# Encoder layer on one core: two weight sums of every seven-product pair made by GpSimd instead of VectorE

## The chip, the core and the metric

One core of a Trainium2 chip runs the whole layer. The metric is the device time of one execution in microseconds (us), the median of three runs. In views of the profile PE is TensorE's matmul side and PEld its weight loads, DVE is VectorE, ACT is ScalarE, POOL is GpSimd, SP is the queue that issues the large loads. All tiles of this kernel have 128 partitions; "128x512" is 512 float32 elements on each.

## The reference

A post-LN encoder layer on 256 tokens of width 2048: LayerNorm, one input projection, two kinds of attention, an output projection with residual and LayerNorm, a SwiGLU FFN of width 5632, residual and a last LayerNorm. What the change touches are the three FFN matrix products:

```python
    h = layer_norm(DEEPNORM_ALPHA * h + mixed, ln1_g[l], ln1_b[l])
    ffn = jnp.einsum('bsf,fd->bsd', jax.nn.silu(jnp.einsum('bsd,df->bsf', h, w_gate[l]))
                     * jnp.einsum('bsd,df->bsf', h, w_up[l]), w_down[l])
    h = layer_norm(DEEPNORM_ALPHA * h + ffn, ln2_g[l], ln2_b[l])
```

## The kernel before

**Precision by splitting.** A float32 operand is split into a rounded high part (`fp32r`, written by ScalarE) and a low part (value minus high part, written by VectorE). One product is then three matmuls: high by high, high by low, low by high. So each weight tile that TensorE takes costs ScalarE a copy and VectorE a subtraction.

**Seven products.** Activations and weights of two successive k-blocks (a "pair": raw tiles r1 and r2 of 128x1024, each halved into two blocks of 512 columns) form a 2x2 by 2x2 block product. Most groups make it of eight block products. In the pairs listed in `SEVEN` and `SEVEN_D` it is made of seven, by a Strassen-Winograd scheme, which needs four sums of weight blocks before the splits. `seven_parts` lists the eleven operations of such a pair:

- `t1` = r1 left + r1 right, and `t3` = r1 right + r2 right, both 128x512, written to the two halves of one tile `t`;
- `t24`: two more sums that read `t` and r2, each 128x512;
- `hi11`, `split_hi`, `hi13`, `hi24`: high parts by ScalarE; `lo11` (128x512), `lo2`, `lo13`, `lo24` (128x1024 each): low parts by VectorE. `hi13` and `lo13` read `t`.

Seven-product pairs are 4 of the 8 pairs of each of ten FFN groups (five "gate" and five "up" groups of 1024 columns, taken in turns: one gate and one up group are a period below) and 12 of the 44 pairs of the down projection, 52 in all. A pair of seven products is 21 matmuls of 128x512, one of eight is 24.

**Order.** Every engine runs its own instructions in the order in which they were emitted, and waits by semaphores. The emission order is made by a planner in the kernel (`Timed`, `Step`, `next_part`): it walks the list of products that TensorE shall take, keeps a clock for each engine with reckoned costs, and emits part operations of the pairs ahead as soon as their engine's reckoned clock is near TensorE's. For GpSimd it reckons `0.1 + n / 400` us, for VectorE `0.07 + n / 960` (n elements per partition). All weight and work tiles come from one pool of 46 slots of 4 KB per partition (`SLOTS`).

**GpSimd's own work.** In the FFN its queue holds only the stores of the FFN's middle activations to DRAM (`mid_d`, from tile `nb`): two 512-column blocks for each of two token tiles per period, each after TensorE has transposed the block and ScalarE has copied it out. They come back as operands of the down projection. Earlier GpSimd makes the reciprocal square roots of the LayerNorms (`rsqrt`: a `TENSOR_SCALAR`, then a `TENSOR_TENSOR` power, tile `rstd`) and issues small loads.

The operations are recorded by a helper class, so that nearly every row of the profile names its line, L53. Rows are told apart by engine, tiles and shape. Buffers of the slot pool are called `sl`, accumulators in PSUM `acc`.

Of the kernel before, what the change touches and what calls it, by code (L numbers as in the profile page):

```python
# [12 lines left out]
ALU = mybir.AluOpType  # L13
# [239 lines left out]
def layer_kernel(ctx: ExitStack, tc: tile.TileContext, A: dict, out: bass.AP):  # L253
    nc = Timed(tc.nc)
# [17 lines left out]
    def slot(shape, dt=F32):  # L272
        t = slab.tile(shape, dt, tag="slab", name=nm("sl"))
        if len(taken) + len(left_over) >= SLOTS and left_over:
            old = min(left_over, key=lambda x: nc.idle(x))
            left_over.remove(old)
            nc.follows(t, old)
        taken.append(t)
        return t
# [5 lines left out]
    def leave(*tiles):  # L285

        for t in tiles:
            taken.remove(t)
            left_over.append(t)
# [3 lines left out]
    def used(key, n, *tiles):  # L293

        uses[key] = uses.get(key, 0) + 1
        if uses[key] == n:
            leave(*tiles)
# [109 lines left out]
    def split_hi(u):  # L407
        wh[u] = slot([P, 1024], F32R)
        nc.scalar.activation(wh[u], raw[u], AF.Copy)

    def split_lo(u):
        wl[u] = slot([P, 1024], F32R)
        nc.vector.tensor_tensor(wl[u], raw[u], wh[u].bitcast(F32), op=ALU.subtract)
# [590 lines left out]
    def op(engine, fn, reads=(), after=(), early=False, takes=0):  # L1004


        return dict(engine=engine, fn=fn, reads=reads, after=after, early=early, takes=takes, done=False)
# [13 lines left out]
    def seven_parts(u):  # L1021

        r1, r2 = raw[u], raw[u + 1]
        s = sums[u] = {}

        def t1():
            s["t"] = slot([P, 2, 512])
            nc.vector.tensor_tensor(s["t"][:, 0], r1[:, :512], r1[:, 512:], op=ALU.add)

        def t3():  # L1030
            nc.vector.tensor_tensor(s["t"][:, 1], r1[:, 512:], r2[:, 512:], op=ALU.add)

        def hi11():
            s["b11"] = slot([P, 2, 512], F32R)
            nc.scalar.activation(s["b11"][:, 0], r1[:, :512], AF.Copy)

        def lo11():
            nc.vector.tensor_tensor(s["b11"][:, 1], r1[:, :512], s["b11"][:, 0].bitcast(F32), op=ALU.subtract)
            leave(r1)

        def hi13():
            s["hi"], s["lo"] = slot([P, 2, 512], F32R), slot([P, 2, 512], F32R)
            nc.scalar.activation(s["hi"], s["t"], AF.Copy)

        def lo13():
            nc.vector.tensor_tensor(s["lo"], s["t"], s["hi"].bitcast(F32), op=ALU.subtract)
            used(("t", u), 2, s["t"])

        def t24():
            s["u"] = slot([P, 2, 512])  # L1050
            nc.vector.tensor_tensor(s["u"][:, 0], s["t"][:, 0], r2[:, 512:], op=ALU.add)
            nc.vector.tensor_tensor(s["u"][:, 1], s["u"][:, 0], r2[:, :512], op=ALU.add)
            used(("t", u), 2, s["t"])
            used(("r2", u), 2, r2)

        def hi24():
            s[2], s[4] = slot([P, 2, 512], F32R), slot([P, 2, 512], F32R)
            nc.scalar.activation(s[2], s["u"], AF.Copy)

        def lo24():  # L1060
            nc.vector.tensor_tensor(s[4], s["u"], s[2].bitcast(F32), op=ALU.subtract)
            leave(s["u"])

        def lo2():
            split_lo(u + 1)
            used(("r2", u), 2, r2)

        return [
            op("act", hi11, lambda: [r1], takes=1),
            op("dve", t1, lambda: [r1], takes=1),  # L1070
            op("dve", t3, lambda: [r1, r2], (1,)),
            op("act", lambda: split_hi(u + 1), lambda: [r2], takes=1),
            op("dve", lo11, lambda: [s["b11"][:, 0]], (0, 1, 2)),
            op("act", hi13, lambda: [s["t"]], (1, 2), takes=2),
            op("dve", t24, lambda: [s["t"]], (1, 2), takes=1),
            op("dve", lo2, lambda: [wh[u + 1]], (3,), takes=1),
            op("act", hi24, lambda: [s["u"]], (6,), takes=2),
            op("dve", lo13, lambda: [s["hi"]], (5,)),
            op("dve", lo24, lambda: [s[2]], (8,)),
        ]  # L1080
# [370 lines left out]
    def prepare(u, seven):  # L1451

        if u not in stages:
            stages[u] = seven_parts(u) if seven else one_parts(u)
            if splits_mid(u):
                add_mid_split(u, stages[u])
            if seven and is_down(u):
                add_mid_sums(u, stages[u])
        return stages[u]
# [165 lines left out]
```

## Time and profile before

| | us |
|---|---|
| median of three runs (lowest, highest) | 1127.96 (1127.65, 1128.34) |
| the profiled execution, its device time | 1127.88 |
| span from its first to its last instruction | 1126.1 |
| FFN with seven-product pairs, from the span's start | 440 to 880.55 |
| down projection | 880.55 to 1086 |
| one gate group and one up group | 83.5 |

The profiled execution's time is its span and 1.8 us around it, and it is 0.08 us from the median. A matmul's duration in the profile overlaps that of the next one, so its start-to-start distance or the count in a stretch tells TensorE's pace, not its busy time. VectorE's records overlap a little in the same way: a record lasts longer than the distance to the next one's start. In the views of stretches overlaps are counted once.

### The profile page before, as it was taken

The page shows a single profiled execution, that of the slowest core. Times are in us where ns is not written, and L with a number is a line of the kernel's source. Part 1 is how long each engine was busy: PE and PEld are TensorE (multiplying, and loading weights), DVE is VectorE, ACT ScalarE, POOL GpSimd, SP SyncE. Part 2 cuts the span into 40 slices and gives each one's busy share as a digit, 9 for nine tenths or more (in the row PEclk, how much of TensorE's full clock was granted, in tenths as well). Part 3 has the DMA queues.
Part 4 walks back from the last instruction along what each step waited for, and adds up shares of the span by engine and source line. Part 5 has one row for each costly group of instructions (what it writes and reads, how often), then busy time and mean ns, then how long its engine had stood idle before and what let it go on. Part 6 is the DMA issues. An engine that isn't in the chain of part 4 may idle for free.

```text
span 1126.1 us, 14151 instructions
## 1 busy us (share of the span) xinstructions
PE 1111.5 (99%) x5032; PEld 904.7 (80%) x5032; DVE 929.0 (83%) x1263; ACT 598.9 (53%) x785; POOL 57.7 (5%) x110
## 2 busy tenths in 40 slices
PE   8999999999999999999999999999999999999998
PEld 4788888888788876888888888888888788878885
DVE  7863876547773669999999999999999999799865
ACT  5552656435563228656556556556567566446640
POOL 2000003110100020000000000000000000000000
PEclk9999999999999999999999999999999999999999
DMA  9664548795766754655754755755756877667741
GB/s 345 233 202 157 166 145 166 183 205 190 159 220 229 243 183 135 211 195 174 269 205 165 278 204 164 280 193 177 271 208 222 286 266 279 218 225 283 250 166 75
DMA packets 70407, 237.15 MB, mean 211 GB/s; under 512 B 8516, under 2 KB 9924, under 8 KB 70336
## 3 DMA queue, kind: packets, MB, share of 16 engines
q1 hardware_dynamic: 65008, 220.49, 57.2%
q0 software_dynamic: 5168, 15.68, 6.8%
q8 instruction: 39, 0.64, 0.2%
q14 instruction: 32, 0.26, 0.1%
q10 hardware_dynamic: 160, 0.08, 0.0%
HBM read 226.25 MB, written 9.97 MB: 210 GB/s over the span
## 4 chain that ended last, share of the span: by engine, by line
PE 49%; issue 41%; DVE 4%; ACT 2%; POOL 2%; DMA 1%; POOLq 0%; ACTq 0%; DVEq 0%
PE acc L53 49%; DVE sl L53 3%; POOL mid_d L53 1%; ACT sl L53 1%; DMA mid_d<-nb 1%; DVE stats L53 1%; ACT s L53 1%; DMA ident<-in_c_ident_dram 0%; DVE s L53 0%; POOL h_d L53 0%; POOL rs L53 0%; DMA sl<-in_w_out_dram 0%; POOL rstd L53 0%; ACT o L53 0%; DVE o L53 0%
## 5 line engine op out<-in xcount | busy, mean ns | idle before, releaser
L53 PE MATMUL acc<-sl,sl 128*128 128x512 f32 (+1 forms) x4676 | 1063.0, 388 | 2.3 <-DVE sl L53 1.4
L53 PEld LDWEIGHTS acc<-sl,sl 128*128 128x128 f32 x4676 | 860.5, 188 | 184.1 <-issue 6.2
L53 DVE TENSOR_TENSOR sl<-sl,sl 128x1024 fp32r<-128x1024 f32 (+3 forms) x710 | 683.1, 1017 | 44.9 <-ACT sl L53 36.6
L53 ACT ACTIVATE sl<-sl 128x1024 fp32r<-128x1024 f32 (+1 forms) x530 | 498.6, 994 | 272.8 <-DVE sl L53 140.8
L53 ACT ACTIVATE sl<-acc 128x256 fp32r<-128x256 f32 (+2 forms) x70 | 33.1, 497 | 91.0 <-PE acc L53 72.4
L53 DVE TENSOR_TENSOR sl<-acc,sl 128x256 fp32r<-128x256 f32 (+2 forms) x94 | 54.8, 596 | 28.2 <-ACT sl L53 21.5
L53 DVE TENSOR_TENSOR sl<-sl 128x512 f32<-128x512 f32 (+1 forms) x76 | 41.4, 558 | 0.3 <-PE acc L53 0.3
L53 DVE SCALAR_TENSOR_TENSOR sl<-sl,acc 128x512 f32<-128x512 f32 x10 | 6.8, 679 | 36.6 <-PE acc L53 36.6
L53 POOL DMA_DIRECT2D mid_d<-nb x22 | 11.9, 540 | 459.1 <-ACT nb L53 459.1
L53 ACT COPY sl<-acc 128x512 f32<-128x512 f32 x31 | 17.1, 588 | 34.3 <-PE acc L53 34.3
L53 ACT COPY nb<-acc 128x512 f32<-128x512 f32 x24 | 14.1, 588 | 35.1 <-PE acc L53 30.3
L53 DVE TENSOR_SCALAR sl<-acc 128x512 f32<-128x512 f32 x8 | 5.5, 688 | 32.7 <-PE acc L53 32.7
L53 ACT ACTIVATE s<-s 128x512 f32<-128x512 f32 x20 | 12.3, 631 | 23.5 <-DVE s L53 23.5
L53 ACT ACTIVATE s<-s,mx 128x256 f32<-128x256 f32 x32 | 15.9, 499 | 15.4 <-DVE mx L53 15.4
L53 POOL DMA_DIRECT2D nb<-in_na_rpb_dram x32 | 19.6, 621 | 85.7 <-DVE s L53 85.7
L53 PE MATMUL acc<-ident,s 128*128 128x128 f32 x136 | 20.5, 273 | 2.5 <-DVE s L53 1.7
L53 PEld LDWEIGHTS acc<-ident,s 128*128 128x128 f32 x136 | 16.5, 140 | 7.5 <-issue 1.9
L53 DVE TENSOR_TENSOR sl<-sl,acc 128x512 f32<-128x512 f32 x16 | 10.6, 681 | 12.7 <-PE acc L53 12.7
L53 PEld LDWEIGHTS acc<-ident,sl 128*128 128x128 f32 x128 | 15.2, 140 | 6.4 <-issue 4.5
L53 DVE BATCH_NORM_STATS2 stats<-sl 128x6 f32<-128x512 f32 x24 | 16.4, 692 | 3.2 <-DMA sl<-in_x_dram 2.6
L53 DVE SCALAR_TENSOR_TENSOR sl<-sl,rstd,sl 128x512 f32<-128x512 f32 x21 | 15.8, 752 | 3.5 <-POOL rstd L53 1.9
L53 DVE SCALAR_TENSOR_TENSOR sl<-sl,mv,sl 128x512 f32<-128x512 f32 x24 | 17.7, 745 | 0.2
(82 smaller groups left out, 226.2 us busy)
## 6 DMA issues: line engine op xcount, KB each, us to landing
sl<-in_w_in_dram SPq DMA_DIRECT2D x96, 512.0 KB, 4.8
sl<-in_w_down_dram SPq DMA_DIRECT2D x88, 512.0 KB, 5.8
sl<-in_w_gate_dram SPq DMA_DIRECT2D x80, 512.0 KB, 4.3
sl<-in_w_up_dram SPq DMA_DIRECT2D x80, 512.0 KB, 4.5
sl<-in_w_out_dram SPq DMA_DIRECT2D x32, 512.0 KB, 5.1
sl<-mid_d SPq DMA_DIRECT2D x14, 512.0 KB, 4.1
mid_d<-nb POOLq DMA_DIRECT2D x22, 256.0 KB, 3.4
sl<-in_w_gate_dram SPq DMA_DIRECT2D x16, 256.0 KB, 4.2
```

The lines of the kernel that those rows point to most:

```text
L53: result = getattr(self.engine, op)(*args, **kw)
```

## The change

`t1` and `t3` of every seven-product pair are issued to GpSimd, and the planner's list names `pool` as their engine, so that it reckons them at GpSimd's cost and on GpSimd's clock. The operands, the tile `t` and the eleven operations stay.

```diff
         def t1():
             s["t"] = slot([P, 2, 512])
-            nc.vector.tensor_tensor(s["t"][:, 0], r1[:, :512], r1[:, 512:], op=ALU.add)
+            nc.gpsimd.tensor_tensor(s["t"][:, 0], r1[:, :512], r1[:, 512:], op=ALU.add)
 
         def t3():
-            nc.vector.tensor_tensor(s["t"][:, 1], r1[:, 512:], r2[:, 512:], op=ALU.add)
+            nc.gpsimd.tensor_tensor(s["t"][:, 1], r1[:, 512:], r2[:, 512:], op=ALU.add)
...
             op("act", hi11, lambda: [r1], takes=1),
-            op("dve", t1, lambda: [r1], takes=1),
-            op("dve", t3, lambda: [r1, r2], (1,)),
+            op("pool", t1, lambda: [r1], takes=1),
+            op("pool", t3, lambda: [r1, r2], (1,)),
```

104 rows leave VectorE's queue (1202 rows before, 1098 now) and join GpSimd's (88 before, 192 now); the other engines keep their numbers of rows.

GpSimd's queue before, where the second period's four stores stand (names are out<-in; `nb` is the copied block):

```order
L53 DMA mid_d<-nb_4821 128x512
L53 DMA mid_d<-nb_5456 128x512
L53 DMA mid_d<-nb_5495 128x512
L53 DMA mid_d<-nb_5522 128x512
L53 DMA mid_d<-nb_5559 128x512
L53 DMA mid_d<-nb_6194 128x512
```

The same place now, from the last pair of one up group to the second pair of the next gate group:

```order
L53 TENSOR_TENSOR sl_5379<-sl_5341 128x512
L53 TENSOR_TENSOR sl_5379<-sl_5341,sl_5343 128x512
L53 DMA mid_d<-nb_5449 128x512
L53 DMA mid_d<-nb_5476 128x512
L53 TENSOR_TENSOR sl_5495<-sl_5431 128x512
L53 TENSOR_TENSOR sl_5495<-sl_5431,sl_5433 128x512
L53 DMA mid_d<-nb_5514 128x512
L53 DMA mid_d<-nb_5543 128x512
L53 TENSOR_TENSOR sl_5595<-sl_5560 128x512
```

The sums `t1` and `t3` of a pair (same output tile, twice) now stand between the stores and after them.

VectorE's queue before, at one seven-product pair in that place (r1 is `sl_5428`, r2 `sl_5430`, `t` is `sl_5511`):

```order
L53 TENSOR_TENSOR sl_5511<-sl_5428 128x512
L53 TENSOR_TENSOR sl_5511<-sl_5428,sl_5430 128x512
L53 TENSOR_TENSOR sl_5483<-sl_5428,sl_5483 128x512
L53 TENSOR_TENSOR sl_5529<-sl_5511,sl_5430 128x512
L53 TENSOR_TENSOR sl_5529<-sl_5529,sl_5430 128x512
L53 TENSOR_TENSOR sl_5549<-sl_5430,sl_5485 128x1024
L53 TENSOR_TENSOR sl_5540<-sl_5511,sl_5539 128x1024
L53 TENSOR_TENSOR sl_5570<-sl_5529,sl_5569 128x1024
```

VectorE's queue now, at the same pair (r1 `sl_5431`, r2 `sl_5433`, `t` `sl_5495`):

```order
L53 TENSOR_TENSOR sl_5493<-sl_5431,sl_5493 128x512
L53 TENSOR_TENSOR sl_5520<-sl_5495,sl_5433 128x512
L53 TENSOR_TENSOR sl_5520<-sl_5520,sl_5433 128x512
L53 TENSOR_TENSOR sl_5532<-sl_5433,sl_5498 128x1024
L53 TENSOR_TENSOR sl_5530<-sl_5495,sl_5529 128x1024
L53 TENSOR_TENSOR sl_5547<-sl_5520,sl_5546 128x1024
```

`t1` and `t3` are gone from the head of the piece; `lo11` leads it, and the second row, the first sum of `t24`, now waits for GpSimd.

## Rows read from the trace of the kernel before

**Rows 1.** The page's busy time, share of the span and instructions of each engine.
```profile
PE 1111.5 (99%) x5032; PEld 904.7 (80%) x5032; DVE 929.0 (83%) x1263; ACT 598.9 (53%) x785; POOL 57.7 (5%) x110
```
**Rows 2.** Stretches: length, busy us and starts of each engine, granted clock, DMA share, GB/s.
```profile
424.00:428.00 4.00, 3.83 (x10) 1.52 (x8) 3.96 (x10) 4.00 (x7) 0.00 (x0) 1.00 0.02 8
...
440.00:880.55 440.55, 440.55 (x1980) 364.25 (x1979) 432.43 (x524) 263.68 (x309) 9.72 (x18) 1.00 0.63 216
...
548.41:631.95 83.54, 83.54 (x378) 69.12 (x377) 81.89 (x99) 49.49 (x59) 2.16 (x4) 1.00 0.61 214
...
880.55:1086.00 205.45, 203.42 (x900) 167.17 (x899) 188.66 (x245) 115.42 (x128) 4.30 (x8) 1.00 0.73 255
```
**Rows 3.** Waits from 440 to 880.55: us in total, times, longest.
```profile
POOL mid_d L53 <- ACT nb L53: 378.8, 18, 80.2
...
DVE sl L53 <- ACT sl L53: 2.6, 5, 0.5
DVE sl L53 <- PE acc L53: 2.3, 5, 0.5
...
PEld acc L53 <- DVE sl L53: 0.4, 2, 0.3
```
**Rows 4.** Waits from 880.55 to 1086.
```profile
DVE sl L53 <- PE acc L53: 8.6, 5, 3.7
DVE sl L53 <- ACT sl L53: 7.1, 9, 1.6
```
**Rows 5.** VectorE from 440 to 880.55 by shape: count, busy us, mean ns of one, idle before.
```profile
L53 DVE TENSOR_TENSOR sl<-sl,sl 128x512 f32<-128x512 f32 x123 | 84.5, 687 | 1.4
...
L53 DVE TENSOR_TENSOR sl<-sl 128x512 f32<-128x512 f32 x41 | 28.1, 684 | 0.0
L53 DVE TENSOR_TENSOR sl<-acc,sl 128x512 f32<-128x512 f32 x30 | 20.7, 689 | 2.8 <-PE acc L53 2.3
L53 DVE TENSOR_TENSOR o<-acc,sl 128x512 f32<-128x512 f32 x19 | 13.0, 686 | 0.5
L53 DVE TENSOR_TENSOR s<-acc,sl 128x512 f32<-128x512 f32 x20 | 12.9, 683 | 0.1
```
**Rows 6.** VectorE in order of time from 562 to 575: start, us, operation.
```profile
564.06 0.69 DVE L53 TENSOR_TENSOR sl<-sl 128x512 f32<-128x512 f32 x1
564.66 8.29 DVE L53 TENSOR_TENSOR sl<-sl,sl 128x512 f32<-128x512 f32 x9
```
**Rows 7.** VectorE and GpSimd in order of time from 404 to 406.5.
```profile
404.57 0.75 DVE L53 SCALAR_TENSOR_TENSOR sl<-sl,mv,sl 128x512 f32<-128x512 f32 x1
404.63 0.74 POOL L53 TENSOR_SCALAR rstd<-mv 128x1 f32<-128x1 f32 x1 [56.39 <-DVE mv L53]
```
**Rows 8.** The same two engines from 18.3 to 19.5.
```profile
18.28 0.63 DVE L53 TENSOR_TENSOR sl<-acc,sl 128x512 fp32r<-128x512 f32 x1
...
18.45 0.19 POOL L53 TENSOR_SCALAR rstd<-mv 128x1 f32<-128x1 f32 x1 [8.11 <-DVE mv L53]
...
18.73 0.55 POOL L53 TENSOR_TENSOR rstd<-rstd,mhalf 128x1 f32<-128x1 f32 x1
...
18.82 0.74 DVE L53 SCALAR_TENSOR_TENSOR sl<-sl,mv,sl 128x512 f32<-128x512 f32 x1
```
**Rows 9.** GpSimd in order of time, two more of the five TENSOR_SCALAR rows.
```profile
414.20 0.74 POOL L53 TENSOR_SCALAR rstd<-mv 128x1 f32<-128x1 f32 x1 [6.47 <-DVE mv L53]
...
1106.37 0.74 POOL L53 TENSOR_SCALAR rstd<-mv 128x1 f32<-128x1 f32 x1 [78.98 <-DVE mv L53]
```
**Rows 10.** GpSimd at the start: the only 128x512 operation it makes, and a 128x1.
```profile
0.72 0.52 POOL L53 MEMSET nb<- 128x512 f32 x1 [0.29 <-POOLq L1610]
1.18 0.10 POOL L53 MEMSET mhalf<- 128x1 f32 x1
```
**Rows 11.** GpSimd from 540 to 645: one period's stores and the next one's first.
```profile
548.41 0.54 POOL L53 DMA_DIRECT2D mid_d<-nb  x1 [80.19 <-ACT nb L53]
552.29 0.54 POOL L53 DMA_DIRECT2D mid_d<-nb  x1 [3.35 <-ACT nb L53]
555.54 0.54 POOL L53 DMA_DIRECT2D mid_d<-nb  x1 [2.71 <-ACT nb L53]
558.87 0.54 POOL L53 DMA_DIRECT2D mid_d<-nb  x1 [2.79 <-ACT nb L53]
631.95 0.54 POOL L53 DMA_DIRECT2D mid_d<-nb  x1 [72.54 <-ACT nb L53]
```

## The prediction

> **What bounds the kernel now.** I read the page's busy shares first [rows 1]: PE is busy 99% of the span, VectorE 83%, GpSimd 5%. On that page the change looks free: work leaves a loaded engine for an idle one. The share over the span misleads, so I then read the stretches in which the moved operations stand [rows 2]. From 440 to 880.55, the FFN, VectorE is busy 432.43 of 440.55 us; 8.1 us are idle, 2%. In the same stretch PE starts 1980 matmuls (transposes among them) in 440.55 us, one in 0.2225 us, and one period of 83.54 us has 378, one in 0.221 us. The pace is constant, so TensorE sets the time. The third view, the waits of that stretch [rows 3], says the same: TensorE waited 0.4 us for VectorE, VectorE 2.3 us for TensorE's accumulators and 2.6 us for ScalarE. So TensorE is the bound and VectorE follows it almost without slack. The reader is to see two things in this. Taking work off VectorE can give back no more than TensorE loses now. Adding work of more than 2% to VectorE makes it the bound. In the down projection (880.55 to 1086) VectorE idles 205.45 - 188.66 = 16.8 us, nearly all of it waiting for TensorE (8.6) and ScalarE (7.1) [rows 4], and TensorE loses 205.45 - 203.42 = 2.0 us.
>
> **What the change removes.** 52 pairs lose two 128x512 additions each on VectorE. A `t1` row starts at 564.06 and the next row at 564.66 [rows 6], so one costs VectorE 0.60 us; its record of 0.68 overlaps the next. 41 of the `t1` rows stand in the FFN stretch [rows 5], 11 behind it. VectorE is relieved of 82 x 0.60 = 49.2 us in the first stretch and 22 x 0.60 = 13.2 us in the second. If that were all, TensorE would gain at most 0.4 us in the first and 2.0 us in the second.
>
> **What it adds to GpSimd.** The trace has no large two-input operation on GpSimd. Nearest rows: a memset of 128x512 takes 0.52 us, one of 128x1 takes 0.10 [rows 10], so a stream of 512 elements per partition costs 0.42; an operation on a tiny tile with an input and an output takes 0.19 when nothing hinders it [rows 8]. An addition reads two such streams and writes one. If the write hides beside the reads, it is 0.19 + 2 x 0.42 = 1.03 us; if all three come after one another, 0.19 + 3 x 0.42 = 1.45 us. I take the middle, 1.24. Even 104 x 1.45 = 151 us are little for an engine that is busy 9.72 + 4.30 = 14 us in the 646 us of both stretches [rows 2]. GpSimd's own time is therefore not the question.
>
> **What it does to VectorE: the step that decides.** In [rows 7] GpSimd's `TENSOR_SCALAR` of 128x1 starts 0.06 us into a VectorE operation with two SBUF inputs, lasts 0.74 us and ends at 405.37, 0.05 us after that operation's end at 405.32. The same instruction takes 0.19 in [rows 8], where VectorE was busy too, but with one of its inputs from PSUM. [Rows 9] have 0.74 twice more. So the two engines share a way into SBUF; a VectorE operation with two SBUF inputs holds it until it ends, and GpSimd waits. What no row shows is the other direction, since every GpSimd operation here reads one or two elements per partition: the VectorE row at 18.82 began beside one and lasted its usual 0.74 [rows 8]. I infer that a way held exclusively by one is also held against it by the other, for as long as GpSimd streams its inputs. Then each moved addition does not relieve VectorE of 0.60 us but takes its time on GpSimd out of VectorE's two-SBUF work. VectorE can meanwhile do only what reads PSUM: 71 rows, 20.7 + 13.0 + 12.9 us and two more rows of 1.4, together 48 of 432 us, 11% [rows 5]. So a moved addition of G us costs VectorE 0.89 G and saves it 0.60. If instead VectorE always won the way, the bill would be alike: its next row in the queue, `t24`, waits for `t`, and it would stand idle there while GpSimd makes both sums.
>
> [...]
>
> **The sum.** FFN: 82 x (0.89 x 1.24 - 0.60) = 41.3 us of new work for VectorE, less the 8.1 us that it idles: TensorE is held up by 33.2 us. Down projection: 22 x 0.504 = 11.1 us, of which I let half of the 16.8 us of idle time take 8.4 (its waits do not lie where the seven-product pairs do): 2.7 us. Together 35.9 us on the profiled 1127.88, 1163.8 us; that execution is 0.08 us from the median, which I neglect. With G at 1.03: 82 x 0.317 - 8.1 = 17.9, and nothing in the down projection: 1146. With G at 1.45: 82 x 0.69 - 8.1 = 48.5 and 22 x 0.69 - 8.4 = 6.8: 1183. If VectorE finds no PSUM work to do while it waits, G at 1.24 gives 82 x 0.64 - 8.1 + 22 x 0.64 - 8.4 = 50, 1178.
>
> **Costed at nothing.** ScalarE's `hi13` now waits for GpSimd; ScalarE is busy 263.68 of 440.55 us [rows 2], and if that cover failed, `lo13` and `lo24` would come late, which is inside the same VectorE bill. Weight loads stay where they are on SP's queue (the same 441 rows) and follow freed slots. TensorE's clock: it is granted 1.00 even from 424 to 428, where only 10 matmuls start in 4 us [rows 2], so short stalls should not cost clock.
>
> **The rivals.**
> *One-way way in.* GpSimd waits for VectorE, but VectorE never for GpSimd, and GpSimd slips in between VectorE's operations. Then an addition is late by at most one VectorE operation and done within some 2.5 us, which the look-ahead covers; VectorE has 49.2 us more room, TensorE keeps its pace: 1127.9, no change. For it: the row at 18.82 was not delayed. Against it: that GpSimd operation read one element, so there was nothing to delay. It decides if VectorE's rows beside GpSimd's additions keep their durations; the border between loss and none is G = (0.60 + 8.1 / 82) / 0.89 = 0.79 us.
> *Relief.* The same, and VectorE's room removes what TensorE loses now: 2.4 us at most, 1125.5.
> *GpSimd's queue.* VectorE is not hindered, but the sums stand behind the stores of `mid_d`, as the order shows, and these wait for ScalarE's copies, 378.8 us in 18 waits [rows 3], 2.7 to 3.4 us apart within a period [rows 11]. Two pairs per period have their sums behind a store. If VectorE stood at `t24` for one such distance for each, it would be 5 x 2 x 2.7 = 27 us; since the planner emits ahead, I price it at half of that, 13 us: 1141. Against it: from 440 to 880.55 VectorE has 49 us of freed time to make such a stall up, and the stall must be longer than the look-ahead.
>
> **How the numbers follow.** Exclusive both ways, 0.80, 1163.8 with its own range 1144 to 1190; one-way, 0.12, 1127.9; the queue alone, 0.05, 1141; relief, 0.03, 1125.5. A change under 0.2%, 2.3 us, is about what three runs of this kernel cannot tell from none. The forecast's own range leaves out some 0.08 (both bounds of G lie in it, the extreme of 1.45 without any PSUM work does not: 82 x 0.85 - 8.1 + 22 x 0.85 - 8.4 = 72, 1200). To leave out no more than 2 in 10 it must reach the one-way case: 1127 to 1190. Relief counts half to faster and half to the same, so faster 0.02, same 0.13; the rest, 0.85, is slower.
>
> **What the next profile would show.** Right: GpSimd has 104 `TENSOR_TENSOR` rows of 128x512 of about 1.0 to 1.5 us, or longer where they include the wait; VectorE's 128x1024 subtractions beside them last longer than 1219 ns or have gaps of about G before them; a period grows from 83.5 to about 90 us with TensorE's waits for VectorE at some 6 us in each; VectorE is idle or stretched, although it has 104 operations less. The gate and up periods carry nearly all of the loss, the projections and attention before 440 none. Wrong: periods of 83.5 us with VectorE's busy time down by 9.6 us in each (one-way), VectorE waiting mostly for GpSimd rows that themselves wait for `nb` (queue), or additions on GpSimd of well over 1.5 us, which would put the time over 1190.

## The result and the profile after

The changed kernel takes 1168.34 us (median of four runs, 1167.22 to 1170.14), against 1127.81 for the kernel before (1127.56 to 1128.34). The ratio is 1.0358, with a 95% interval of 1.0345 to 1.0371. The profiled execution took 1167.22 us with a span of 1165.4, 39.3 us more than before. One execution of one experiment below, the last, ran at a granted clock of 0.556 and took 1883.71 us; it is in a slow state and left out.

The page's line of busy shares, which answers to [rows 1]:

```profile
PE 1128.4 (97%) x5032; PEld 910.9 (78%) x5032; DVE 966.0 (83%) x1159; ACT 600.6 (52%) x785; POOL 251.5 (22%) x214
```

VectorE makes 104 operations less and is busy 37 us more. That is the result in one line. The same stretches as in [rows 2], moved to where they now lie (FFN, its second period, down projection):

```profile
440.00:916.58 476.58, 456.25 (x1986) 370.66 (x1985) 462.23 (x442) 265.01 (x309) 161.61 (x101) 0.98 0.58 201
556.50:646.36 89.86, 86.21 (x378) 69.94 (x377) 87.68 (x83) 49.91 (x58) 31.30 (x20) 0.98 0.57 199
916.58:1125.00 208.42, 203.46 (x893) 166.90 (x892) 195.51 (x222) 115.82 (x128) 43.83 (x30) 0.99 0.72 251
```

The FFN is 476.58 - 440.55 = 36.0 us longer, the down projection 208.42 - 205.45 = 3.0, and the end 0.3; nothing is lost before 440. VectorE's idle time in the FFN is 476.58 - 462.23 = 14.4 us, 3% of the stretch, and TensorE's idle time there is 476.58 - 456.25 = 20.3 us where it had none: VectorE now sets the time, and no longer TensorE.

VectorE in the FFN by shape, as in [rows 5] (count, busy us, mean ns, idle before). First the row of the kernel before for 1024 columns, then the changed kernel's:

```profile
L53 DVE TENSOR_TENSOR sl<-sl,sl 128x1024 fp32r<-128x1024 f32 x214 | 248.0, 1219 | 2.6 <-ACT sl L53 2.6
...
L53 DVE TENSOR_TENSOR sl<-sl,sl 128x1024 fp32r<-128x1024 f32 x214 | 310.2, 1503 | 8.4 <-ACT sl L53 8.2
L53 DVE TENSOR_TENSOR sl<-sl,sl 128x512 f32<-128x512 f32 x82 | 68.9, 840 | 1.4
L53 DVE TENSOR_TENSOR sl<-sl,sl 128x512 fp32r<-128x512 f32 x45 | 34.0, 755 | 0.0
L53 DVE TENSOR_TENSOR sl<-acc,sl 128x512 f32<-128x512 f32 x30 | 20.5, 685 | 1.8 <-PE acc L53 1.0 <-ACT sl L53 0.5
L53 DVE TENSOR_TENSOR o<-acc,sl 128x512 f32<-128x512 f32 x19 | 13.0, 684 | 0.1
```

Of these groups those that read only SBUF are longer (1024 columns: 1219 ns before, 1503 now; the 512-column sums: 687 before, 840 now). The rows that read PSUM kept their 0.68 to 0.69 us. The new rows of GpSimd in the same stretch, `t1` and `t3`:

```profile
L53 POOL TENSOR_TENSOR sl<-sl 128x512 f32<-128x512 f32 x41 | 80.9, 1974 | 226.4 <-PE acc L53 115.0 <-DVE sl L53 59.4 <-DMA sl<-in_w_up_dram 40.7
L53 POOL TENSOR_TENSOR sl<-sl,sl 128x512 f32<-128x512 f32 x41 | 74.3, 1813 | 20.6 <-DMA sl<-in_w_up_dram 13.7 <-DMA sl<-in_w_gate_dram 5.9 <-DMA sl<-in_w_down_dram 1.0
```

These means hold waiting inside an instruction: unhindered, a sum takes 1.28 to 1.30 us. One place shows both engines in order of time (start, us). First GpSimd, where two sums run unhindered from 560.27 and two hindered from 570.50:

```profile
559.71 0.54 POOL L53 DMA_DIRECT2D mid_d<-nb  x1 [2.65 <-ACT nb L53]
560.27 1.30 POOL L53 TENSOR_TENSOR sl<-sl 128x512 f32<-128x512 f32 x1
561.53 1.28 POOL L53 TENSOR_TENSOR sl<-sl,sl 128x512 f32<-128x512 f32 x1
...
570.50 2.18 POOL L53 TENSOR_TENSOR sl<-sl 128x512 f32<-128x512 f32 x1 [3.60 <-DMA sl<-in_w_gate_dram]
572.63 2.29 POOL L53 TENSOR_TENSOR sl<-sl,sl 128x512 f32<-128x512 f32 x1
```

And VectorE beside them:

```profile
559.99 3.91 DVE L53 TENSOR_TENSOR sl<-sl,sl 128x1024 fp32r<-128x1024 f32 x1
...
571.43 4.56 DVE L53 TENSOR_TENSOR sl<-sl,sl 128x1024 fp32r<-128x1024 f32 x2
...
573.68 2.31 DVE L53 TENSOR_TENSOR sl<-sl,sl 128x1024 fp32r<-128x1024 f32 x1
```

The line of 571.43 holds two rows and ends at 575.99, and the second is the row at 573.68; each lasts about 2.3 us instead of 1.22. The VectorE row in progress at 570.50 started at 570.29 and ends at 571.51 by its record of 1.22; the sum ends at 572.68, 1.17 us later; the VectorE row of 571.43, whose record is 2.33, ends at 573.76, 1.08 us after the sum; and the second sum and row end at 574.92 and 575.99. So I read these rows as turns: the sum waits until the VectorE row in progress is over, the next VectorE row until the sum is over, and a sum takes 2.33 - 1.22 = 1.11 us out of VectorE's time. At 559.99 both sums of a pair came one right after the other, and one VectorE row waited for both: 3.91 us, 2.7 us more than alone.

The waits of the FFN stretch, first VectorE's, then those of TensorE's weight loads, beside [rows 3]:

```profile
DVE sl L53 <- ACT sl L53: 10.7, 7, 2.0
DVE sl L53 <- PE acc L53: 1.0, 1, 1.0
...
PEld acc L53 <- DVE s L53: 14.9, 9, 2.3
PEld acc L53 <- DVE sl L53: 10.4, 8, 2.3
```

In these two lines TensorE's weight loads wait 25.3 us for VectorE (0.4 before). No VectorE row of the stretch is listed as waiting for a GpSimd row: what VectorE loses to GpSimd lies inside its rows. But VectorE itself waits 10.7 us for ScalarE (2.6 before), which the prediction did not expect.

### The profile page after: what moved, and what is told of

The parts are those of the page before. It is cut to its first block, busy times and chain, and to the rows that moved or that the text cites. A ratio compares the mean times of both kernels' runs of the same rounds, so it can differ in the third digit from the quotient of the medians.

```text
span 1165.4 us, 14287 instructions
## 1 busy us (share of the span) xinstructions
PE 1128.4 (97%) x5032; PEld 910.9 (78%) x5032; DVE 966.0 (83%) x1159; ACT 600.6 (52%) x785; POOL 251.5 (22%) x214
## 4 chain that ended last, share of the span: by engine, by line
PE 46%; DVE 10%; issue 5%; ACT 1%; DMA 1%; POOL 0%; DVEq 0%; ACTq 0%; POOLq 0%
PE acc L53 46%; DVE sl L53 8%; DVE s L53 1%; ACT sl L53 1%; DMA mid_d<-nb 1%; DVE stats L53 0%; POOL sl L53 0%; DVE o L53 0%; ACT nb L53 0%; DVEq L53 0%; ACT rows L53 0%; DVE mv L53 0%; ACTq L53 0%; DVE rstd L53 0%; POOLq L53 0%
## 5 line engine op out<-in xcount | busy, mean ns | idle before, releaser
L53 PE MATMUL acc<-sl,sl 128*128 128x512 f32 (+1 forms) x4676 | 1078.2, 391 | 22.3 <-DVE sl L53 10.9
L53 DVE TENSOR_TENSOR sl<-sl,sl 128x1024 fp32r<-128x1024 f32 (+3 forms) x658 | 744.0, 1187 | 47.4 <-ACT sl L53 42.4
L53 POOL TENSOR_TENSOR sl<-sl 128x512 f32<-128x512 f32 x52 | 103.2, 1985 | 339.2 <-PE acc L53 176.2
L53 POOL TENSOR_TENSOR sl<-sl,sl 128x512 f32<-128x512 f32 x52 | 91.9, 1767 | 22.5 <-DMA sl<-in_w_up_dram 13.7
L53 ACT ACTIVATE sl<-acc 128x256 fp32r<-128x256 f32 (+2 forms) x70 | 33.2, 497 | 92.1 <-PE acc L53 73.5
L53 POOL TENSOR_SCALAR rstd<-mv 128x1 f32<-128x1 f32 x5 | 2.6, 523 | 131.2 <-DVE mv L53 131.2
L53 DVE TENSOR_TENSOR sl<-sl,acc 128x512 f32<-128x512 f32 x16 | 10.6, 681 | 13.7 <-PE acc L53 13.6
```

The costliest lines, as they stand in the source:

```text
L53: result = getattr(self.engine, op)(*args, **kw)
```

## The experiments

All FFN stretches below run from 440 to the first of the last four stores of `mid_d`, as the 880.55 and 916.58 above. "Lengthening" is VectorE's busy time in that stretch, less what it would be with every row at its length of before. In the changed kernel it is 462.23 - (432.43 - 82 x 0.60) = 79.0 us, 0.963 us for each of the 82 sums. In the code, `nc.nc` issues an operation without the planner's reckoning it, so that the order of all others stays, and `nc.note` lets the planner reckon one without issuing it.

**Is it the sums' reading of SBUF, or a wait for their results?** The kernel before, unchanged, with GpSimd repeating both sums into a tile that nobody reads:

```diff
+    extra = const.tile([P, 512], mybir.dt.bfloat16, name="extra")
...
             nc.vector.tensor_tensor(s["t"][:, 0], r1[:, :512], r1[:, 512:], op=ALU.add)
+            nc.nc.gpsimd.tensor_tensor(extra, r1[:, :512], r1[:, 512:], op=ALU.add)
...
             nc.vector.tensor_tensor(s["t"][:, 1], r1[:, 512:], r2[:, 512:], op=ALU.add)
+            nc.nc.gpsimd.tensor_tensor(extra, r1[:, 512:], r2[:, 512:], op=ALU.add)
```

> The kernel before, with GpSimd making t1 and t3 a second time into a scratch tile (float32 inputs, bfloat16 output, 128x512) that nobody reads; VectorE keeps its own t1 and t3. Exclusive way into SBUF: no instruction waits for the sums, yet VectorE's two-input rows beside them last about 1.1 us longer; at the 0.96 us per addition that the changed kernel shows, 82 x 0.96 - 8.1 = 71 us in the FFN and 22 x 0.92 - 8.4 = 12 us in the down projection, so 1205 to 1225 us. Queue (the loss comes from VectorE waiting for sums that stand behind the stores): 1128 us. One-way way in: 1128 us.

Measured: 1217.66 us, ratio 1.0794 (1.0778 to 1.0811). The FFN:

```profile
440.00:959.58 519.58, 474.89 (x1983) 378.05 (x1982) 514.08 (x523) 262.45 (x310) 162.60 (x99) 0.93 0.55 184
```

VectorE does the work of before and is busy 514.08 - 432.43 = 81.7 us more, against a lengthening of 79.0 in the changed kernel. Nothing uses the results of these sums, no `t24` and no `hi13`. So the loss can be made by GpSimd's work beside VectorE's alone, without any wait for its results.

The same places, with GpSimd busy but reading next to nothing (a copy of 128x1 and three memsets of 128x512 for each sum):

```diff
+            nc.nc.gpsimd.tensor_copy(extra[:, :1], r1[:, 512:513])
+            for _ in range(3):
+                nc.nc.gpsimd.memset(extra, 0.0)
```

> The kernel before, with GpSimd busy at the same places for about as long (a 128x1 copy from r1 or r2, then three 128x512 memsets of a scratch tile, 104 times) but reading next to nothing. If VectorE is held only against GpSimd's reading: 1128 us within 3 us, and VectorE's 128x1024 rows keep their 1219 ns. If any GpSimd access to SBUF holds VectorE: as extra_adds, 1200 us or more.

Measured: 1127.59 us, ratio 0.9998 (0.9988 to 1.0007). By shape, FFN:

```profile
L53 DVE TENSOR_TENSOR sl<-sl,sl 128x1024 fp32r<-128x1024 f32 x213 | 246.6, 1217 | 2.6 <-ACT sl L53 2.6
...
L1039 POOL MEMSET extra<- 128x512 bf16 x123 | 64.6, 525 | 7.1
L1033 POOL MEMSET extra<- 128x512 bf16 x120 | 63.0, 525 | 7.0
L1037 POOL CAST extra<-sl 128x1 bf16<-128x1 f32 x41 | 34.1, 831 | 16.4 <-DMA sl<-in_w_gate_dram 13.8 <-DMA sl<-in_w_up_dram 0.3
```

GpSimd was busy 191 us in the FFN, more than with the sums (162.6), and VectorE's rows kept 1217 ns. The writing did no harm here (ratio 0.9998) and neither did GpSimd's being busy; the additions, which read SBUF at length, did (1.0794). All of them have two inputs; a long operation with one input was not run. The small copies show the other side: in this listing one element takes a mean of 831 ns, against 0.46 us for the copy at 470.53.

**How does the loss grow?** Only `t3` moved:

```diff
-            nc.vector.tensor_tensor(s["t"][:, 1], r1[:, 512:], r2[:, 512:], op=ALU.add)
+            nc.gpsimd.tensor_tensor(s["t"][:, 1], r1[:, 512:], r2[:, 512:], op=ALU.add)
...
-            op("dve", t3, lambda: [r1, r2], (1,)),
+            op("pool", t3, lambda: [r1, r2], (1,)),
```

> Half the change: t3 on GpSimd, t1 on VectorE. The sum on record (1.10 us cost, 0.60 saved): 41 x 0.504 - 8.1 = 12.6 us, 1140. The same at the measured 0.96 per addition: 41 x 0.36 - 8.1 = 6.7 us, 1135. If the delay is in proportion to the number of additions (VectorE's idle time does not absorb any): half of 40.5, 1148. One-way: 1128.

Measured: 1136.88 us, ratio 1.0085 (1.0068 to 1.0101), a loss of 9.0 us. In the FFN (449.37 us) VectorE is busy 443.46, so the lengthening is 443.46 - (432.43 - 24.6) = 35.6 us, 0.87 for each of 41 sums, and the idle time 5.9. Half of the sums cost less than a quarter of the loss, since both terms are under half of the changed kernel's: busy +11.0 and idle -2.2 here, busy +29.8 and idle +6.2 there. Of the times expected, 1135, from the measured price, came nearest.

And VectorE overloaded by its own work, without GpSimd (`t3` made a second time by VectorE into the spare tile):

```diff
+            nc.nc.vector.tensor_tensor(extra, r1[:, 512:], r2[:, 512:], op=ALU.add)
```

> The kernel before, with VectorE making t3 twice (the second into a scratch tile), nothing moved to GpSimd: VectorE gets 41 x 0.60 = 24.6 us more work in the FFN, near the 29.8 us by which its busy time grew there in the changed kernel. If VectorE's idle time absorbs first, as the sum on record has it: 24.6 - 8.1 = 16.5 us, 1144. If an overloaded VectorE also idles more, as in the changed kernel (busy +29.8, delay +36.0): about 24.6 + 6 = 31 us, 1158.

Measured: 1148.34 us, ratio 1.0183 (1.0168 to 1.0198). This lies between the two times expected. The FFN:

```profile
440.00:899.47 459.47, 445.06 (x1978) 362.57 (x1977) 453.93 (x561) 261.03 (x309) 9.72 (x18) 1.00 0.60 207
```

It takes 18.9 us more, with VectorE busy 21.5 us more. So most of VectorE's additional work does become time, which is the premise of the whole sum. Of its 8.1 us of idle time, only 2.6 took up work.

**Do the stores on GpSimd's queue matter?** The changed kernel with the stores of `mid_d` on SP's queue:

```diff
-        nc.gpsimd.dma_start(mid_d[c * P : (c + 1) * P, t * 512 : (t + 1) * 512], f)
+        nc.sync.dma_start(mid_d[c * P : (c + 1) * P, t * 512 : (t + 1) * 512], f)
```

> The changed kernel with the mid_d stores issued from SP's queue, so that no sum on GpSimd stands behind a store. If contention for the way into SBUF is the whole of it: 1168 within 5 us, and VectorE still idles some 14 us from 440 to the end of the FFN. If sums held up behind stores make VectorE and ScalarE wait: 1160 or less, VectorE's idle time back to about 6 us.

Measured: 1154.96 us, ratio 1.0245 (1.0229 to 1.0261), 13.4 us less than the changed kernel. Its FFN:

```profile
440.00:902.70 462.70, 446.85 (x1982) 364.43 (x1981) 448.98 (x439) 263.72 (x308) 159.77 (x84) 1.00 0.61 205
```

VectorE is busy 13.2 us less than in the changed kernel and idle 13.7, much as there (14.4). The time is that of the second expectation, the idle time that of the first. So the stores do not cost a wait of VectorE; they cost lengthening. The pair whose sums ran at 560.27 in the changed kernel (its 21st and 22nd sums) shows how; GpSimd, then VectorE:

```profile
552.73 2.15 POOL L53 TENSOR_TENSOR sl<-sl 128x512 f32<-128x512 f32 x1 [6.40 <-DVE sl L53]
554.84 1.72 POOL L53 TENSOR_TENSOR sl<-sl,sl 128x512 f32<-128x512 f32 x1
...
554.36 1.07 DVE L53 TENSOR_TENSOR s<-s,o 128x512 f32<-128x512 f32 x1
555.35 0.68 DVE L53 TENSOR_TENSOR o<-acc,sl 128x512 f32<-128x512 f32 x1
556.06 1.05 DVE L53 TENSOR_TENSOR s<-s,o 128x512 f32<-128x512 f32 x1
```

Without the store ahead of them the sums run while every other VectorE row reads PSUM, and each lengthens a row from 0.69 to about 1.06 only, 0.37 us. Behind the store they run after those rows are over, back to back, and one VectorE row loses 2.7 us. Counted over the trace, the changed kernel has five VectorE rows in the FFN that are lengthened by 2.7 us (3.84 to 3.93 instead of 1.22), about one period apart and each with both sums right behind a store; this kernel has none. Row by row against the lengths of before, the lengthening falls from 79.1 to 67.8 us: those five rows are 13.3 us of it, and all others together grow by 2.0, among them nine rows between PSUM reads by some 0.37 each. The other 2 us of the 13.2 are no gain: three rows fewer start in this stretch (439 against 442). The planner's order moved slightly too (in each period a 512-wide and a 1024-wide VectorE row changed places), and its part was not separated.

**Where does VectorE's new wait for ScalarE come from?** First guess: the planner reckons GpSimd too cheap. Its cost for GpSimd doubled:

```diff
-                cost = 0.1 + n / 400
+                cost = 0.1 + n / 200
```

> The changed kernel with the planner reckoning GpSimd's operations at 0.1 + n / 200 us, 2.66 for an addition of 512 (the trace has 1.3 to 2.4), so that VectorE's and ScalarE's rows that read the sums are put later. If the 6 us by which VectorE's idle time grew come from rows put too early behind late sums: idle falls from 14.4 to 6 to 8 us and the time to about 1161. If the idle time comes from the gate groups' ends, where VectorE is behind anyway: no change, 1168 within 3 us.

Measured: 1172.53 us, ratio 1.0401 (1.0383 to 1.0418), slower still, and outside both expectations; VectorE waits 11.2 us for ScalarE. The guess is wrong. Second guess: the planner takes VectorE for emptier by two operations for each pair, though each moved sum still takes VectorE's time, and therefore draws other rows forward. Here GpSimd makes the sums, but the planner books them as VectorE's, which leaves the order of all other rows as before the change (against the changed kernel; `t3` likewise):

```diff
-            nc.gpsimd.tensor_tensor(s["t"][:, 0], r1[:, :512], r1[:, 512:], op=ALU.add)
+            nc.nc.gpsimd.tensor_tensor(s["t"][:, 0], r1[:, :512], r1[:, 512:], op=ALU.add)
+            nc.note("dve", "tensor_tensor", [s["t"][:, 0]], [r1[:, :512], r1[:, 512:]])
...
-            op("pool", t1, lambda: [r1], takes=1),
-            op("pool", t3, lambda: [r1, r2], (1,)),
+            op("dve", t1, lambda: [r1], takes=1),
+            op("dve", t3, lambda: [r1, r2], (1,)),
```

> The two sums are issued to GpSimd, but the planner reckons them as VectorE's, so that all other engines keep the order of the kernel before and VectorE's queue only loses the 104 rows. If the idle time that VectorE gained (14.4 us from 440 to the end of the FFN against 8.1) comes from an order made for an emptier VectorE: idle 8 us or less and about 1161 us. If it comes from sums that are late: idle stays at 14 us or more and the time at 1168 or above. The contention itself stays in both, VectorE's 128x1024 rows at a mean near 1500 ns.

Measured: 1157.45 us, ratio 1.0263 (1.0246 to 1.028), 10.9 less than the changed kernel. The FFN and VectorE's wait for ScalarE in it:

```profile
440.00:905.85 465.85, 451.62 (x1980) 367.26 (x1980) 460.24 (x441) 262.41 (x309) 154.09 (x101) 0.99 0.61 205
...
DVE sl L53 <- ACT sl L53: 1.6, 3, 0.5
```

The lengthening is nearly the same, 460.24 - (432.43 - 49.2) = 77.0 us; the idle time falls from 14.4 to 5.6, and the wait for ScalarE from 10.7 to 1.6. So these 9 us came with the planner's new order, not with a late sum. Both repairs in one kernel, this order and the stores on SP's queue:

> The same with the mid_d stores from SP's queue, so that the sums stand behind no store. If what the stores cost (13 us in the changed kernel) is the place they give the sums: about 1148. If the two gains are the same gain: 1155.

Measured: 1149.91 us, ratio 1.0197 (1.0182 to 1.0212). FFN 458.60 us, VectorE busy 455.01, idle 3.6, lengthening 71.8. The gains do not add up: moving the stores is worth 7.5 us here and 13.4 above. It is the fastest of the versions with both sums on GpSimd, and still 22 us slower than the kernel before.

**Is the first sum's 10.9 us a cost of starting up?** In the changed kernel the first sum lasts 10.91 us, at 437.77. With one addition of 128x1 on GpSimd at the start of the kernel:

```diff
     nc.gpsimd.memset(mhalf, -0.5)
+    warm_add = const.tile([P, 1], F32, name="warm_add")
+    nc.nc.gpsimd.tensor_tensor(warm_add, mhalf, mhalf, op=ALU.add)
```

> The changed kernel with one 128x1 addition on GpSimd right after the start. If the first large addition took 10.91 us because its code had to be loaded: that row falls to 1.3 to 2.4 us and the kernel gains 3 to 5 us, 1164. If GpSimd was kept out by VectorE's rows: the row stays near 10.9 us and the time at 1168.

Measured: 1166.78 us (median of the other three), ratio 1.0344 (1.0327 to 1.0361), and the first large sum lasts 10.90 us, as in the changed kernel. So it is not a cost that a small addition ahead of it takes away.

## Why the prediction was right, and where its terms were off

**Which engine would become the bound: right.** The loss lies where VectorE had 2% of slack [rows 2], and the experiment with VectorE's own extra work shows that most of the added work there turns into time (18.9 of 21.5 us).

**Exclusive both ways: right, and now shown.** The trace of before had only GpSimd as the one that waits [rows 7]. The rows at 570 to 576 show VectorE waiting (2.33 us instead of 1.22), and the two experiments with extra work on GpSimd (ratio 1.0794 with the sums, 0.9998 with the memsets) leave its long reads of SBUF as the cause; whether two inputs are needed was not run. That whoever comes first holds the way does not fit the five places with 3.84 to 3.93 us: there VectorE's row starts 0.20 to 0.30 us before the first sum, by the records (0.28 at 559.99), and yet waits for both. The rivals without this, no change at 1127.9 and relief at 1125.5, are refuted by the first experiment alone.

**The VectorE bill per sum (0.89 G, forecast 1.10 us): mis-sized, measured 0.963.** G was taken as 1.24, between 1.03 and 1.45. An unhindered sum is recorded at 1.28 to 1.30, but it keeps VectorE out for only 1.11 of them (1.22 becomes 2.33). 0.89 x 1.11 = 0.99 would have been close to 0.963; that the share of rows that read PSUM is the reason was not tested. Over the 82 sums the step is 82 x 1.1036 - 79.0 = 11.5 us too large.

**Less the 8.1 us that it idles: wrong, and by more.** I let all of VectorE's idle time take up the new work. It grew by 6.2 us instead. Even without GpSimd only 2.6 of the 8.1 were filled; and the planner's new order added waits for ScalarE. The step is 14.3 us too small. The two errors nearly cancel: 33.2 us forecast for the FFN, 36.0 measured. In the down projection busy time grew by 6.9 us, of which idle time took 3.9: 3.0 measured, 2.7 forecast, where the terms were 11.1 and 8.4. The good total of 1163.8 is therefore partly luck.

**Costed at nothing, first: ScalarE.** I wrote that if its cover failed, the cost would be inside the same VectorE bill. It was not inside. VectorE waited 8.1 us more for ScalarE; the price was the order's, since in the kernel that keeps the old order ScalarE still waits 20.1 us for GpSimd's sums and VectorE only 1.6 for ScalarE.

**Costed at nothing, second: TensorE's clock.** "Short stalls should not cost clock" did not hold in the changed kernel, as far as the order of time tells: the granted clock fell there behind three stalls, from 1.00 to 0.66. Stretches of 5 us of the changed kernel (as in [rows 2], the granted clock third from the end):

```profile
600.00:605.00 5.00, 2.04 (x7) 0.97 (x6) 5.00 (x7) 0.63 (x1) 3.35 (x2) 1.00 0.20 80
605.00:610.00 5.00, 4.31 (x12) 3.41 (x13) 3.36 (x5) 4.93 (x7) 0.00 (x0) 0.66 0.34 105
...
695.00:700.00 5.00, 4.46 (x11) 3.50 (x12) 3.36 (x4) 5.00 (x7) 0.00 (x0) 0.50 0.35 93
```

And what TensorE did before the first of them, in order of time:

```profile
600.66 0.53 PEld L53 LDWEIGHTS acc<-sl,sl 128*128 128x128 f32 x3 [0.97 <-DVE s L53]
...
602.87 0.53 PEld L53 LDWEIGHTS acc<-sl,sl 128*128 128x128 f32 x3 [1.69 <-DVE sl L53]
...
605.69 2.30 PEld L53 LDWEIGHTS acc<-sl,sl 128*128 128x128 f32 x7 [2.29 <-DVE s L53]
```

Three waits of 0.97, 1.69 and 2.29 us for VectorE stand close together at the end of a gate group, seven matmuls start in the 5 us from 600, and the granted clock falls from 1.00 in these to 0.66 in the next 5 us; from 695 to 700 it is 0.50. In the stretch of [rows 2] with 10 matmuls in 4 us it stayed at 1.00. That the stalls make it fall, no run shows by itself. What the fall adds to the time is not settled, but three things speak for little. VectorE is the bound there and waits only 1.0 us for TensorE in the whole FFN. The kernel with GpSimd's extra sums has the lowest granted clock in its FFN, 0.93, and VectorE idles only 519.58 - 514.08 = 5.5 us there, less than in the kernel before. And the kernel with both repairs has a granted clock of 1.00 over its FFN and still loses 18 us there. No run took the clock's part away alone.

**The queue behind the stores: a part of the loss, not a rival to it.** Priced at 13 us as a stall of VectorE at `t24`, it was put down as something that acts if VectorE is not hindered. Moving the stores away gave 13.4 us, but by another way, so that the equal numbers are chance: the stores decide when the sums run, and so which VectorE rows they hold.

**The signs.** 104 sums, a period of 89.86 us for the forecast "about 90", longer 1024-wide rows and nothing lost before 440: all as written. One sign was badly chosen: sums "well over 1.5 us" were to mean a time over 1190. The means of `t1` and `t3` were 1.97 and 1.81 in the FFN, since a record holds the wait too (2.18 at 570.50, 1.30 at 560.27); only VectorE's lengthening tells the price.

## What to carry to other kernels

A low busy share of GpSimd (5% here) was no offer: before moving work to it, ask which of VectorE's rows have both inputs in SBUF (here the mean of the 1024-column ones grew from 1219 to 1503 ns, while those that read PSUM kept their 0.68 to 0.69 us), and charge each sum's time to VectorE, not to GpSimd. Here VectorE gave up 0.60 us of work and lost 0.96 us for it. If such work must lie on GpSimd, put it where every other VectorE row reads PSUM (0.37 us lost instead of 1.1), keep waiting stores out of its queue, and look at the order that a planner makes when it takes VectorE for emptier (9 us of idle time here). And do not spend all of an engine's idle time in a sum: only a third of VectorE's 8.1 us was filled by VectorE's own work.

## What the runs showed of the hardware that was not expected

At 570.50 GpSimd got in at the end of the VectorE row in progress, but that is not always so. At the first sum it was kept out for some 9.6 us, an estimate: 10.91 less the 1.30 of an unhindered sum (GpSimd, then VectorE's longest piece beside it):

```profile
437.77 10.91 POOL L53 TENSOR_TENSOR sl<-sl 128x512 f32<-128x512 f32 x1 [16.21 <-DVE sl L53]
...
439.02 7.57 DVE L53 TENSOR_TENSOR sl<-sl,sl 128x1024 fp32r<-128x1024 f32 x8
```

Eight VectorE rows ran in a stretch of 7.57 us while it waited. A copy of 128x1 at about the same place, in the experiment that only writes, took 10.69 us; in the kernel that keeps the old order the first sum comes at 446.37 and takes 2.44. What lets VectorE keep the way for many rows there, and gives it up after one row elsewhere, stays open; so does why, behind a store, it yields to two sums in a row, the first of which started 0.28 us after VectorE's row (560.27 and 559.99).
